# Side-by-side token parts: two matmuls where three stood, and PSUM as four pairs of banks

## The chip, the cores and the metric

The kernel runs on one core of one Trainium2 chip. The metric is the device time of one execution in microseconds (us). The kernel before was timed three times: 933.48, 933.98 and 934.42, a median of 933.98 us. Engines are named as in the profile: PE multiplies matrices (PEld is its loading of the stationary operand, which overlaps PE), DVE and ACT are the two elementwise engines, POOL does some small powers, and SP issues the transfers.

## The reference, cut to what matters

The input is 256 tokens of 1024 features in float32. A first block runs a SwiGLU feed-forward, a token mixer (retention and neighbourhood attention) and a second feed-forward; a second block runs a gated linear recurrence and a gated short convolution. Nearly all the work is in products with weights that are read once:

```python
def _swiglu(x, w_in, w_out):
    g, u = jnp.split(x @ w_in, 2, axis=-1)
    return (jax.nn.silu(g) * u) @ w_out

def first_block(x, ...):
    h = _swiglu(_rms_norm(x, ffn1_pre_norm), ffn1_w_in, ffn1_w_out)     # 1024 -> 2 x 2816 -> 1024
    x = x + 0.5 * _rms_norm(h, ffn1_post_norm)
    x = x + _rms_norm(_token_mixing(_rms_norm(x, mix_pre_norm), w_mix_in, ...), mix_post_norm)
    h = _swiglu(_rms_norm(x, ffn2_pre_norm), ffn2_w_in, ffn2_w_out)
    return x + 0.5 * _rms_norm(h, ffn2_post_norm)

def second_block(x, ...):
    x = x + recurrent_mixer(rmsnorm(x, norm_g[0]), a_w_in, ...)   # 1024 -> 2 x 1536 -> 1024
    x = x + shortconv_mixer(rmsnorm(x, norm_g[1]), b_w_in, ...)   # 1024 -> 4 x 1536 -> 1024
    return rmsnorm(x, final_g)
```

## The kernel before, in words

Every float32 operand of a large product is held as two float32r parts, hi (a rounded copy) and lo (the rest), and a product is three matmuls: hi by hi, hi by lo and lo by hi. The helper `mm3` (lines 222 to 226) issues them for one stationary and one moving pair.

Weights come in parts of 128 by 1024 (512 KB), 300 of which are split: a transfer on SP's queue (L75) fills `raw`, ACT copies `raw` to `hi` (L87), and DVE subtracts to get `lo` (L88). The parts lie in a ring of 41 slots of 4 KB a partition; a part is split up to 15 parts ahead of its use when the ring has room.

A block has two phases. In `phase_a` a unit of 256 output features is made feature-major: the weights are stationary and the 256 tokens are the moving columns (`mm_a2`, 16 calls of `mm3` a unit, 256 columns each, into one PSUM bank). The normed input is a `Pair`: tiles `ph` and `pl`, four K-tiles of 256 tokens to a slot. The first units of a phase are taken token-major instead (`mm_tok`: tokens stationary, 256 weight columns moving) and turned by PE afterwards. In `phase_b` tokens are stationary and 512 columns of weights move (`mm_b`), into four accumulator banks. The token mixer also uses 512 moving columns for its token-major products (`mm_t`).

At the end of a unit the block's `evac` reads the bank: in the feed-forward ACT takes Silu of the gate's bank (L471), DVE multiplies it by the other bank (L472), and `split_pair` makes the next pair (L450, L451). At the joint between blocks the new normed input `hn` is turned by PE and split by `transpose_pair` (L346, L350, L351): four tiles of 128 columns to a bank, one ACT copy and one DVE subtraction of 512 columns for each bank. PSUM is a pool of eight tiles of one bank each.

The program is written in order and a scheduler, fed by a model of the engines, sets the order of each engine's instructions when it is built; an engine runs its own list in that order. In the mixer, DVE adds a mask to four bias tables `t2` (L603), which come by 16 small transfers of `in_na_rel_bias`, and turns queries and keys by position (`rope`, L568 to L573) before PE transposes them (`turn`, L581). In the recurrent block `conv` (L937, L942) reads the bank of a unit, `gates` (L912) multiplies its result by the gate weights, and `finish` (L1004 to L1011) ends in the pairs that `phase_b` reads.

Of the kernel before, what the change touches and what calls it, by code (L numbers as in the profile page):

```python
# [49 lines left out]
class Stream:  # L50
    """Weights in the order of their use: loaded ahead, then split into two float32r parts."""
# [72 lines left out]
def block_kernel(ctx: ExitStack, tc: tile.TileContext, A, C, out):  # L124
# [63 lines left out]
    add(u_ag[:EARLY] + [ax[0], ax[1], u_gw[0], ax[2], u_gw[1], ax[3], ax[4], u_gw[2], ax[5]] + u_ag[EARLY:])  # L188
# [33 lines left out]
    def mm3(ps, a, b, first, last):  # L222
        """ps += a[0]+a[1] times b[0]+b[1], each a pair of float32r parts (stationary, moving)."""
# [4 lines left out]
    class Pair:  # L228
        """A feature-major activation in two float32r parts, by tiles of 128 features."""

        def __init__(self, nk):
            self.nk, self.gone = nk, 0
            self.h, self.l = [], []

        def slots(self, k):
            while k // 4 >= len(self.h):
                self.h.append(S.slot(F32R, "ph"))
                self.l.append(S.slot(F32R, "pl"))

        def at(self, k, t0=0, t1=SEQ):  # L240
            o = (k % 4) * SEQ
            return self.h[k // 4][:, o + t0:o + t1], self.l[k // 4][:, o + t0:o + t1]

        def view(self, part, k, n):
            self.slots(k)
            t = (self.h if part == 0 else self.l)[k // 4]
            o = (k % 4) * SEQ
            return t[:, o:o + n * SEQ].rearrange("p (k t) -> p k t", k=n)

        def used(self, k):  # L250
            """Tiles up to k are done with."""
            while self.gone <= (self.nk - 1) // 4 and (k >= 4 * self.gone + 3 or k == self.nk - 1):
                S.drop(2)
                self.gone += 1
# [3 lines left out]

    def mm_a2(bk, u, xt):
        """bk[features, (half, token)] for the 256 columns of u."""  # L260
        for m in range(2):
            c = slice(m * 128, (m + 1) * 128)
            for q, p in enumerate(u.parts):
                if m == 0:
                    S.use(p)
                for j in range(p.a):
                    k = q * p.a + j
                    mm3(bk[:, m * SEQ:(m + 1) * SEQ], (p.hi[:, j, c], p.lo[:, j, c]), xt.at(k),
                        k == 0, k == u.a - 1)
                if m == 1:  # L270
                    S.done(p)

    def mm_tok(bk, u, xt, t):
        """bk[token of tile t, (t, 256 columns)]"""
# [10 lines left out]
    def mm_t(ps, p, xt, t, k0, nk):  # L285
        """ps[token of tile t, 512 columns], the tiles of K in p"""
# [4 lines left out]
    def columns(*cuts):  # L291
        """accumulators (bank, columns) of a token tile"""
        return [(bank()[:, :b - a], slice(a, b)) for a, b in zip(cuts, cuts[1:])]

    def mm_b(acc, p, xt, t, k, nk):
        """the columns of acc of token tile t, tile k of K"""
# [4 lines left out]
    def inv_rms(a, b, eps):  # L301
        """(a + b + eps) ** -0.5"""
# [37 lines left out]
    def transpose_pair(src, t, pair, k0, n):  # L340
        """n tiles of 128 columns of the token-major src become tiles k0.. of pair, tokens t."""
        for b in range(0, n, 4):
            ps = bank()
# [3 lines left out]
            pv = ps[:, :m * 128].rearrange("p (k t) -> p k t", k=m)  # L347
            h = pair.view(0, k0 + b, m)[:, :, t * 128:(t + 1) * 128]
            lo = pair.view(1, k0 + b, m)[:, :, t * 128:(t + 1) * 128]
            act.activation(out=h, in_=pv, func=AF.Copy)  # L350
            dve.tensor_tensor(out=lo, in0=pv, in1=h.bitcast(F32), op=ALU.subtract)  # L351

    class Next:
        """What a block hands over: its normed input, one token tile after the other."""
# [26 lines left out]
        # (tile, part, columns): the last parts by columns, so that the first columns' sum of  # L381
        # squares runs under the others' products
# [21 lines left out]
    def phase_a(us, nxt, evac, late, tok_evac=None):  # L404
        """feature-major products of the normed input. The first units are taken token-major, token
        tile 0 first, so that the second tile's norm runs under the first's products."""
# [8 lines left out]
        for i, u in enumerate(us):  # L415
# [3 lines left out]
            else:  # L419
                b = bank()  # L420
# [10 lines left out]
    def turn_tok(src):  # L431
        """[token, (tile, 256 features)] to a bank [feature, (half, token)]."""
# [7 lines left out]
    def turn_evac(evac):  # L440
        def first(i, b):
            s = tmp()
            act.activation(out=s, in_=b, func=AF.Copy)
            return lambda: evac(i, turn_tok(s))
        return first

    def split_pair(pair, k, n, src):
        """src [128, n, 256] becomes tiles k..k+n of pair."""
        h, lo = pair.view(0, k, n), pair.view(1, k, n)
# [11 lines left out]
    def ffn(us, nxt, post, next_ap, late, aside=None):  # L461
# [3 lines left out]
        def evac(i, b):  # L465
            if i % 2 == 0:
                held[i] = b
                return
            g = held.pop(i - 1)
            sg = tmp()  # L470
            act.activation(out=sg, in_=g, func=AF.Silu)  # L471
            dve.tensor_tensor(out=sg, in0=sg, in1=b, op=ALU.mult)  # L472
            split_pair(f, i - 1, 2, two(sg))
# [3 lines left out]
        def tok_evac(i, b):  # L477
# [7 lines left out]
            return lambda: split_pair(f, i - 1, 2, two(turn_tok(sg)))  # L485
# [36 lines left out]
    def mixing(nxt):  # L522
        dist = S.slot(F32, "dist")
        S.fetch(dist, C["dist"])
        # rows of the mirrored bias, one further to the right for each query: keys in falling order
# [9 lines left out]
        # queries and keys of the retention, token-major, turned by their positions  # L535
        xt = nxt.pair
        acc = [[bank(), bank()] for _ in range(2)]
# [13 lines left out]
        # decay[m, t] between key m and query t  # L551
# [35 lines left out]
        # neighbourhood queries and keys, feature-major  # L587
        nqk = [S.slot(F32, "nqk") for _ in range(2)]

        def full_a(u, xt):  # L590
            b = bank()
            mm_a2(b, u, xt)
            return b

        for i, u in enumerate(u_nq + u_nk):
            b = full_a(u, xt)
            act.activation(out=nqk[i // 2][:, (i % 2) * 512:(i % 2 + 1) * 512], in_=b, func=AF.Copy,
                           scale=ND ** -0.5 if i < 2 else 1.0)
            turn(roped[i // 2][i % 2], i // 2, i % 2)
# [5 lines left out]
        # scores of the retention, [key, query], weighted by the decay  # L605
# [10 lines left out]
        # scores of the neighbourhood attention, [query, key]  # L616
# [4 lines left out]
        def na_scores(hh, i):  # L621
# [6 lines left out]
            pb = [bank(), bank()]  # L628
# [22 lines left out]
        def full_t(us, xt, evac, between):  # L651
            ps = [bank(), bank()]
# [16 lines left out]
        def bt_nv(i):  # L669
            na_scores(0, i)  # L670
# [27 lines left out]
        def na_turn(h):  # L698
# [8 lines left out]
            if hl == 3:  # L707
                S.drop(2)      # prob
# [6 lines left out]
        def na_pv(h):  # L715
            if h == 0:
                na_o.extend([bank(), bank()])
# [5 lines left out]
            if h % 2:  # L723
                S.drop()       # pt
# [9 lines left out]
        # the retention's output, token-major, normed by heads  # L734
# [4 lines left out]
        def ret_y(t):  # L739
            for hp in range(2):  # L740
                ps = bank()
# [43 lines left out]
        S.drop(4)      # rp, v  # L785
# [11 lines left out]
        def o_turn(i):  # L797
# [3 lines left out]
            pv = ps.rearrange("p (k t) -> p k t", k=4)  # L801
            h, lo = (ot.view(z, 0, 4)[:, :, i * 128:(i + 1) * 128] for z in range(2))
            act.activation(out=h, in_=pv, func=AF.Copy)
            dve.tensor_tensor(out=lo, in0=pv, in1=h.bitcast(F32), op=ALU.subtract)

        for i, u in enumerate(u_gn + u_gr):
            S.reserve = 6 if i < 6 else 4
            b = full_a(u, xt)
# [342 lines left out]
```

## Time and profile before

| what | value |
|---|---|
| median of three runs | 933.98 us |
| the profiled execution, first to last instruction (its span) | 934.7 us |
| PE busy | 910.2 us, 97% of the span |
| PEld busy | 852.6 us, 91% |
| DVE busy | 555.1 us, 59% |
| ACT busy | 470.0 us, 50% |
| PE's share of the chain that ended last | 85% |

The profiled execution has only its span as a time; it is 0.7 us longer than the median. Matmuls overlap in the pipeline, so what one costs is the distance from its start to the next one's start, not the duration in its row.

### The profile page before, as it was taken

What the parts mean: (1) busy time and instruction counts of PE and PEld (TensorE: products, weight loads), DVE (VectorE), ACT (ScalarE), POOL (GpSimd) and SP (SyncE); (2) the same over time, 40 slices, a digit from 0 to 9 for tenths busy, and PEclk for the clock granted to TensorE, in tenths of its full rate; (3) what the DMA queues carried; (4) which work ended last, traced back from release to release, by engine and by line L of the source; (5) the groups of instructions that cost most, each with busy time, mean ns of one, the idle gap of its engine ahead of it and who ended that gap; (6) DMA issues with size and microseconds to landing.
All of it is one profiled execution on the core that took longest, in us unless ns stands there. A gap on an engine that the chain in (4) does not pass through costs nothing.

```text
span 934.7 us, 15517 instructions
## 1 busy us (share of the span) xinstructions
PE 910.2 (97%) x6374; PEld 852.6 (91%) x6374; DVE 555.1 (59%) x714; ACT 470.0 (50%) x662; POOL 13.9 (1%) x24
## 2 busy tenths in 40 slices
PE   5999999999999999999999999999999999999997
PEld 5999998888978899998999999889998889999986
DVE  5774555556936463667574446545787965756512
ACT  6664545443746454545454444534769845544401
POOL 0000000000000000000000000000000000000000
PEclk9999999999999999999999999999999999999999
DMA  9964547747527443666555546767426745655401
GB/s 299 328 209 158 175 158 251 264 116 199 190 86 247 126 150 131 225 201 222 164 182 164 159 165 211 238 190 245 139 91 204 246 154 183 221 163 182 158 1 46
DMA packets 132442, 169.21 MB, mean 181 GB/s; under 512 B 12048, under 2 KB 112148, under 8 KB 132372
## 3 DMA queue, kind: packets, MB, share of 16 engines
q1 hardware_dynamic: 132372, 168.23, 55.8%
q8 instruction: 50, 0.82, 0.4%
q14 instruction: 20, 0.16, 0.1%
HBM read 167.16 MB, written 1.05 MB: 180 GB/s over the span
## 4 chain that ended last, share of the span: by engine, by line
PE 85%; DVE 5%; ACT 4%; DMA 2%; SPq 2%; issue 2%; POOL 0%; DVEq 0%; POOLq 0%; ACTq 0%
PE bank L224 27%; PE bank L226 27%; PE bank L225 27%; DVE lo L88 2%; SPq L116 1%; DMA t<-in_na_rel_bias 1%; DMA raw<-in_ffn_w_in 1%; DVE ri L1008 1%; ACT hi L87 1%; PE bank L721 1%; PE bank L746 1%; ACT ri L949 1%; ACT u L948 0%; PE bank L436 0%; PE bank L632 0%
## 5 line engine op out<-in xcount | busy, mean ns | idle before, releaser
L88 DVE TENSOR_TENSOR lo<-raw,hi 128x1024 fp32r<-128x1024 f32 x300 | 358.9, 1221 | 132.2 <-ACT hi L87 79.8
L87 ACT ACTIVATE hi<-raw 128x1024 fp32r<-128x1024 f32 x300 | 307.0, 1055 | 172.7 <-PE bank L226 69.2
L224 PE MATMUL bank<-ph,hi 128*128 128x256 f32 x1360 | 387.3, 285 | 0.0
L225 PE MATMUL bank<-pl,hi 128*128 128x256 f32 x1360 | 384.9, 283 | 0.0
L226 PE MATMUL bank<-ph,lo 128*128 128x256 f32 x1360 | 384.8, 283 | 0.0
L225 PEld LDWEIGHTS bank<-pl,hi 128*128 128x128 f32 x1360 | 261.0, 192 | 0.2
L224 PEld LDWEIGHTS bank<-ph,hi 128*128 128x128 f32 x1360 | 261.0, 192 | 0.2
L226 PEld LDWEIGHTS bank<-ph,lo 128*128 128x128 f32 x1360 | 261.0, 192 | 0.0
L224 PE MATMUL bank<-hi,ph 128*128 128x512 f32 (+1 forms) x636 | 225.4, 356 | 4.2 <-ACT ph L350 4.2
L225 PE MATMUL bank<-lo,ph 128*128 128x512 f32 (+1 forms) x636 | 223.5, 353 | 0.2 <-DVE lo L88 0.2
L226 PE MATMUL bank<-hi,pl 128*128 128x512 f32 (+1 forms) x636 | 221.7, 353 | 1.9 <-DVE pl L351 1.8
L224 PEld LDWEIGHTS bank<-hi,ph 128*128 128x128 f32 x636 | 121.4, 191 | 23.2 <-ACT ph L350 6.5
L226 PEld LDWEIGHTS bank<-hi,pl 128*128 128x128 f32 x636 | 120.4, 191 | 18.4 <-DVE pl L351 2.6
L225 PEld LDWEIGHTS bank<-lo,ph 128*128 128x128 f32 x636 | 121.4, 191 | 15.8 <-DVE lo L88 0.5
L450 ACT ACTIVATE ph<-tmp 128x512 fp32r<-128x512 f32 x28 | 17.6, 629 | 57.5 <-DVE tmp L472 52.8
L313 ACT ACTIVATE tmp<-x 128x512 f32<-128x512 f32 (+1 forms) x25 | 15.2, 609 | 41.6 <-DVE x L328 34.5
L472 DVE TENSOR_TENSOR tmp<-tmp,bank 128x512 f32<-128x512 f32 x19 | 13.0, 685 | 34.5 <-PE bank L226 34.5
L451 DVE TENSOR_TENSOR pl<-tmp,ph 128x512 fp32r<-128x512 f32 x28 | 19.1, 689 | 12.9 <-ACT ph L450 12.9
L304 DVE TENSOR_SCALAR small<-small 128x1 f32<-128x1 f32 x18 | 3.8, 210 | 34.6 <-ACT tmp L332 28.4
L351 DVE TENSOR_TENSOR pl<-bank,ph 128x512 fp32r<-128x512 f32 x24 | 15.8, 684 | 13.5 <-ACT ph L350 13.5
L306 POOL TENSOR_TENSOR small<-small,half 128x1 f32<-128x1 f32 x18 | 11.7, 650 | 809.8 <-DVE small L304 809.8
L321 DVE SCALAR_TENSOR_TENSOR hn<-x,small,g 128x512 f32<-128x512 f32 x24 | 17.0, 748 | 9.8 <-POOL small L306 6.6
(135 smaller groups left out, 413.4 us busy)
## 6 DMA issues: line engine op xcount, KB each, us to landing
raw<-in_ffn_w_in SPq DMA_DIRECT2D x88, 512.0 KB, 5.2
raw<-in_w_mix_in SPq DMA_DIRECT2D x52, 512.0 KB, 4.5
raw<-in_b_w_in SPq DMA_DIRECT2D x48, 512.0 KB, 4.4
raw<-in_ffn_w_out SPq DMA_DIRECT2D x44, 512.0 KB, 4.3
raw<-in_a_w_in SPq DMA_DIRECT2D x24, 512.0 KB, 4.3
raw<-in_a_w_out SPq DMA_DIRECT2D x12, 512.0 KB, 3.7
raw<-in_b_w_out SPq DMA_DIRECT2D x12, 512.0 KB, 4.0
raw<-in_w_ret_out SPq DMA_DIRECT2D x8, 512.0 KB, 4.3
```

The lines of the kernel that those rows point to most:

```text
L87: self.copied = self.nc.scalar.activation(out=p.hi, in_=p.raw, func=AF.Copy)
L88: self.nc.vector.tensor_tensor(out=p.lo, in0=p.raw, in1=p.hi.bitcast(F32), op=ALU.subtract)
L224: pe.matmul(ps, a[0], b[0], start=first, stop=False)
L225: pe.matmul(ps, a[0], b[1], start=False, stop=False)
L226: pe.matmul(ps, a[1], b[0], start=False, stop=last)
L306: nc.gpsimd.tensor_tensor(out=r, in0=v, in1=half[:, 0:1], op=ALU.pow)
L313: act.activation(out=tmp()[:, :c1 - c0], in_=x[:, t, c0:c1], func=AF.Square, scale=1.0 / 32, accum_out=ss[:, c:c + 1])
L321: dve.scalar_tensor_tensor(out=hn[:, s], in0=x[:, t, s], scalar=r, in1=g[:, s], op0=ALU.mult, op1=ALU.mult)
L351: dve.tensor_tensor(out=lo, in0=pv, in1=h.bitcast(F32), op=ALU.subtract)
L450: act.activation(out=h, in_=src, func=AF.Copy)
L451: dve.tensor_tensor(out=lo, in0=src, in1=h.bitcast(F32), op=ALU.subtract)
L472: dve.tensor_tensor(out=sg, in0=sg, in1=b, op=ALU.mult)
```

## The change: what it does

A `Pair` now keeps the hi and the lo tokens of one K-tile side by side: 256 hi columns and then 256 lo columns, two K-tiles to a slot. `mm_wide` passes a stationary hi weight block over all 512 of them in one matmul, and the lo weight block over the 256 hi columns in a second. The two halves of the result, weights by hi tokens and hi weights by lo tokens, lie in the two halves of a bank, so a unit needs two banks; `total` sums the halves when the unit is evicted, with one ACT copy and one DVE addition into an SBUF tile, and what followed reads that tile. PSUM is a pool of four tiles of two banks; code that wants single banks takes halves of a pair. The ring has 40 slots instead of 41, the pool `tmp` eight tiles instead of six. `transpose_pair` splits two tiles at a time instead of four. In the mixer the transposes of the turned queries and keys come two units later; in the recurrent block the gates come one unit later.

```diff
-RING = 41          # slots of 4 KB a partition
+RING = 40
-    tp = ctx.enter_context(tc.tile_pool(name="tmp", bufs=6))
+    tp = ctx.enter_context(tc.tile_pool(name="tmp", bufs=8))
-    pp = ctx.enter_context(tc.tile_pool(name="psum", bufs=8, space=PSUM))
+    pp = ctx.enter_context(tc.tile_pool(name="psum", bufs=4, space=PSUM))
+    spare = []
+    def double():
+        return pp.tile([128, 2, 512], F32, tag="b", name="bank")
+    def banks2():
+        b = double()
+        return [b[:, 0, :], b[:, 1, :]]
     def bank():
-        return pp.tile([128, 512], F32, tag="b", name="bank")
+        if not spare:
+            spare.extend(banks2())
+        return spare.pop(0)
...
+        def both(self, k):
+            o = (k % 2) * 512
+            return self.s[k // 2][:, o:o + 512]
...
+    def mm_wide(b, w, xt, k, first, last):
+        hi, lo = w
+        pe.matmul(b, hi, xt.both(k), start=first, stop=False, skip_group_check=True)
+        pe.matmul(b[:, 0:SEQ], lo, xt.at(k)[0], start=False, stop=last, skip_group_check=True)
...
     def mm_a2(bk, u, xt):
...
-                    mm3(bk[:, m * SEQ:(m + 1) * SEQ], (p.hi[:, j, c], p.lo[:, j, c]), xt.at(k),
-                        k == 0, k == u.a - 1)
+                    mm_wide(bk[:, m, :], (p.hi[:, j, c], p.lo[:, j, c]), xt, k, k == 0, k == u.a - 1)
...
+    def total(out, bk, scale=None):
+        v = bk.rearrange("p m (z t) -> p m z t", z=2)
+        o = two(out)
+        if scale is None:
+            act.activation(out=o, in_=v[:, :, 1, :], func=AF.Copy)
+            dve.tensor_tensor(out=o, in0=v[:, :, 0, :], in1=o, op=ALU.add)
...
     def transpose_pair(src, t, pair, k0, n):
-        for b in range(0, n, 4):
-            ps = bank()
+        for b, ps in zip(range(0, n, 4), banks2()):
...
+            for j in range(0, m, 2):
+                pv = ps[:, j * 128:(j + 2) * 128].rearrange("p (k t) -> p k t", k=2)
+                h, lo = (pair.view(z, k0 + b + j)[:, :, t * 128:(t + 1) * 128] for z in range(2))
...
         def evac(i, b):                      # feed-forward
             if i % 2 == 0:
-                held[i] = b
+                held[i] = total(tmp(), b)
+                act.activation(out=held[i], in_=held[i], func=AF.Silu)
                 return
-            g = held.pop(i - 1)
-            sg = tmp()
-            act.activation(out=sg, in_=g, func=AF.Silu)
-            dve.tensor_tensor(out=sg, in0=sg, in1=b, op=ALU.mult)
+            sg, u = held.pop(i - 1), total(tmp(), b)
+            dve.tensor_tensor(out=sg, in0=sg, in1=u, op=ALU.mult)
...
         for i, u in enumerate(u_nq + u_nk):  # token mixer
-            b = full_a(u, xt)
...
-            turn(roped[i // 2][i % 2], i // 2, i % 2)
+            full_a(u, xt, nqk[i // 2][:, (i % 2) * 512:(i % 2 + 1) * 512], ND ** -0.5 if i < 2 else None)
+            if i > 1:
+                turn(roped[0][i - 2], 0, i - 2)
...
-        def evac(i, b):                      # recurrent block
+        def evac(i, b, turned=False):
             j = i - EARLY
-            conv(j, b)
-            if j:
-                S.todo.append(partial(sigmoids, j - 1, gates(j - 1)))
+            conv(j, b if turned else total(tmp(), b))
+            if j > 1:
+                S.todo.append(partial(sigmoids, j - 2, gates(j - 2)))
...
             b = double()
             mm_a2(b, u, xt)
-            banks.append(b)
-            if j == 0:
-                S.todo.append(partial(sigmoids, 5, gates(5)))
+            banks.append(total(tmp(), b))
+            if j < 2:
+                S.todo.append(partial(sigmoids, 4 + j, gates(4 + j)))
```

PE's list in a feed-forward unit, before: `hi` and `lo` are the weights (stationary), `ph` and `pl` the token parts (moving), and 128x256 is the output.

```order
L224 MATMUL bank_606<-ph_123,hi_400 128x256
L225 MATMUL bank_606<-pl_124,hi_400 128x256
L226 MATMUL bank_606<-ph_123,lo_401 128x256
L224 MATMUL bank_606<-ph_123,hi_400 128x256
L225 MATMUL bank_606<-pl_124,hi_400 128x256
L226 MATMUL bank_606<-ph_123,lo_401 128x256
```

And in such a unit now, where `pr` holds both token parts:

```order
L279 MATMUL bank_492<-pr_133,hi_374 128x512
L280 MATMUL bank_492<-pr_133,lo_375 128x256
L279 MATMUL bank_492<-pr_133,hi_374 128x512
L280 MATMUL bank_492<-pr_133,lo_375 128x256
L279 MATMUL bank_492<-pr_136,hi_374 128x512
L280 MATMUL bank_492<-pr_136,lo_375 128x256
```

Two matmuls stand for three; the program has 1360 such pairs where it had 1360 such triples, and all other matmuls are as many as before.

DVE's list where the token mixer begins, before: L603 adds the mask to a bias table, L351 subtracts for `pl` of the second token tile (its eight K-tiles in two instructions), L88 splits weights, L555 begins the decay tables.

```order
L603 TENSOR_TENSOR t2_2174<-t2_2174,mask_79 128x768
L351 TENSOR_TENSOR pl_2119<-bank_2264,ph_2118 128x4x128
L351 TENSOR_TENSOR pl_2128<-bank_2271,ph_2127 128x4x128
L603 TENSOR_TENSOR t2_2175<-t2_2175,mask_79 128x768
L88 TENSOR_TENSOR lo_2201<-raw_2079,hi_2200 128x1024
L88 TENSOR_TENSOR lo_2207<-raw_2091,hi_2206 128x1024
```

The same place now (L637 is the mask, L387 the subtraction, in four instructions for the second token tile, L590 the decay tables):

```order
L637 TENSOR_TENSOR t2_1910<-t2_1910,mask_79 128x768
L88 TENSOR_TENSOR lo_1933<-raw_1810,hi_1932 128x1024
L637 TENSOR_TENSOR t2_1911<-t2_1911,mask_79 128x768
L387 TENSOR_TENSOR pr_1861<-bank_1994,pr_1861 128x2x128
L88 TENSOR_TENSOR lo_1939<-raw_1822,hi_1938 128x1024
L88 TENSOR_TENSOR lo_1949<-raw_1828,hi_1948 128x1024
L590 TENSOR_SCALAR decay_2059<-dist_1906,lg_96 128x512 x2
L590 TENSOR_SCALAR decay_2060<-dist_1906,lg_96 128x512 x2
L387 TENSOR_TENSOR pr_1864<-bank_1994,pr_1864 128x2x128
```

The last two subtractions of the second token tile (K-tiles 4 to 7) stood ahead of the last mask and now stand behind it, the very last one also behind two splits and four decay instructions.

## Rows read from the trace of the kernel before

**Rows 1.** Page, part 1: busy time, share of the span, count.

```profile
PE 910.2 (97%) x6374; PEld 852.6 (91%) x6374; DVE 555.1 (59%) x714; ACT 470.0 (50%) x662; POOL 13.9 (1%) x24
```

**Rows 2.** Page, part 4: the chain that ended last, by engine.

```profile
PE 85%; DVE 5%; ACT 4%; DMA 2%; SPq 2%; issue 2%; POOL 0%; DVEq 0%; POOLq 0%; ACTq 0%
```

**Rows 3.** Groups by shape: busy us, mean ns of one, idle us before it.

```profile
L224 PE MATMUL bank<-ph,hi 128*128 128x256 f32 x1360 | 387.3, 285 | 0.0
...
L88 DVE TENSOR_TENSOR lo<-raw,hi 128x1024 fp32r<-128x1024 f32 x300 | 358.9, 1221 | 132.2 <-ACT hi L87 79.8 <-PE bank L225 33.2 <-issue 15.0
```

**Rows 4.** Timeline of PE, 59.8 to 64: start, duration, line, operation.

```profile
59.77 0.28 PE L225 MATMUL bank<-pl,hi 128*128 128x256 f32 x1
...
63.97 0.28 PE L224 MATMUL bank<-ph,hi 128*128 128x256 f32 x1
```

**Rows 5.** Timeline of PE, 599.7 to 602.

```profile
599.66 0.39 PE L226 MATMUL bank<-hi,pl 128*128 128x512 f32 x1
...
601.93 0.39 PE L224 MATMUL bank<-hi,ph 128*128 128x512 f32 x1
```

**Rows 6.** Timeline of PE, 896 to 898, where widths change.

```profile
896.42 0.39 PE L226 MATMUL bank<-hi,pl 128*128 128x512 f32 x1
896.65 0.28 PE L224 MATMUL bank<-hi,ph 128*128 128x256 f32 x1
...
897.24 0.28 PE L226 MATMUL bank<-hi,pl 128*128 128x256 f32 x1
897.36 0.40 PE L224 MATMUL bank<-hi,ph 128*128 128x512 f32 x1
```

**Rows 7.** Timeline of PE, 442 to 444: float32 transposes.

```profile
442.23 0.93 PE L346 MATMUL bank<-ident,hn 128*128 128x128 f32 x7
```

**Rows 8.** Waits of PE: us in total, times, longest.

```profile
PE bank L224 <- ACT ph L350: 4.2, 9, 1.1
PE bank L226 <- DVE pl L351: 1.8, 2, 1.0
PE bank L581 <- DVE tmp L573: 1.6, 1, 1.6
PE bank L912 <- DVE u L942: 0.9, 1, 0.9
```

**Rows 9.** Groups by shape: instructions like the added ones.

```profile
L350 ACT ACTIVATE ph<-bank 128x512 fp32r<-128x512 f32 x24 | 13.1, 594 | 17.3 <-PE bank L346 17.3
L472 DVE TENSOR_TENSOR tmp<-tmp,bank 128x512 f32<-128x512 f32 x19 | 13.0, 685 | 34.5 <-PE bank L226 34.5
...
L328 DVE TENSOR_TENSOR x<-bank,x 128x256 f32<-128x256 f32 x2 | 0.8, 424 | 1.0 <-PE bank L226 1.0
L313 ACT ACTIVATE tmp<-x 128x256 f32<-128x256 f32 x2 | 0.8, 418 | 1.4 <-DVE x L328 1.4
```

**Rows 10.** Timeline of PE, 203 to 232: the token mixer's first product.

```profile
205.37 0.50 PE L224 MATMUL bank<-hi,ph 128*128 128x512 f32 x1 [0.45 <-ACT ph L350]
```

**Rows 11.** Timeline of DVE, 218 to 232: in brackets the idle time before.

```profile
218.85 0.96 DVE L603 TENSOR_TENSOR t<-t,mask 128x768 f32<-128x768 f32 x1 [0.40 <-DMA t<-in_na_rel_bias]
...
225.97 0.96 DVE L603 TENSOR_TENSOR t<-t,mask 128x768 f32<-128x768 f32 x1 [4.96 <-DMA t<-in_na_rel_bias]
226.84 3.48 DVE L88 TENSOR_TENSOR lo<-raw,hi 128x1024 fp32r<-128x1024 f32 x3
230.25 1.66 DVE L555 TENSOR_SCALAR decay<-dist,lg 128x512 f32<-128x512 f32 x4
```

**Rows 12.** Timeline of PE, 695 to 718: recurrent block.

```profile
695.57 1.68 PE L912 MATMUL bank<-u,raw 128*128 128x256 f32 x7
...
717.47 0.40 PE L224 MATMUL bank<-hi,ph 128*128 128x512 f32 x1
```

**Rows 13.** Timeline of DVE, 703 to 735: recurrent block.

```profile
703.54 0.86 DVE L942 SCALAR_TENSOR_TENSOR u<-bank,vec_a,u 128x253 f32<-128x253 f32 x2
...
729.02 1.89 DVE L451 TENSOR_TENSOR pl<-tmp,ph 128x512 fp32r<-128x512 f32 x3
```

More of the change, by code (lines that the diff above doesn't have):

```diff
@@ L232, in __init__, with slot, view @@
             self.nk, self.gone = nk, 0
[L233 to L238, printed above, removed]
-        def at(self, k, t0=0, t1=SEQ):
[L241 to L248, printed above, removed]
+            self.s = []
+        def slot(self, k):
+            while k // 2 >= len(self.s):
+                self.s.append(S.slot(F32R, "pr"))
+            return self.s[k // 2]
+        def at(self, k, t0=0, t1=SEQ):
+            t, o = self.s[k // 2], (k % 2) * 512
+            return t[:, o + t0:o + t1], t[:, o + SEQ + t0:o + SEQ + t1]
+        def both(self, k):
+            o = (k % 2) * 512
+            return self.s[k // 2][:, o:o + 512]
+        def view(self, part, k):
+            return self.slot(k).rearrange("p (k z t) -> p k z t", k=2, z=2)[:, :, part, :]
         def used(self, k):
-            while self.gone <= (self.nk - 1) // 4 and (k >= 4 * self.gone + 3 or k == self.nk - 1):
-                S.drop(2)
+            while self.gone <= (self.nk - 1) // 2 and (k >= 2 * self.gone + 1 or k == self.nk - 1):
+                S.drop()
                 self.gone += 1
@@ L291, in columns @@
     def columns(*cuts):
-        return [(bank()[:, :b - a], slice(a, b)) for a, b in zip(cuts, cuts[1:])]
+        bs = banks2()
+        if len(cuts) > 3:
+            bs += banks2()
+        return [(ps[:, :b - a], slice(a, b)) for ps, a, b in zip(bs, cuts, cuts[1:])]
     def mm_b(acc, p, xt, t, k, nk):
@@ L419, in phase_a @@
             else:
-                b = bank()
+                b = double()
                 mm_a2(b, u, xt)
@@ L484, in tok_evac @@
             dve.tensor_tensor(out=sg, in0=sg, in1=b, op=ALU.mult)
[L485 removed]
+            return lambda: split_pair(f, i - 1, two(turn_tok(sg)))
         xt = phase_a(us[0], nxt, evac, late, tok_evac)
@@ L536, in mixing @@
         xt = nxt.pair
-        acc = [[bank(), bank()] for _ in range(2)]
+        acc = [banks2() for _ in range(2)]
         qk_units = [u_rq, u_rk]
@@ L627, in na_scores @@
             tv = [t2[2 * hh + q][:, :768].rearrange("p (h r c) -> p h r c", h=2, r=6) for q in range(2)]
-            pb = [bank(), bank()]
+            pb = banks2()
             for hl in range(4):
@@ L651, in full_t @@
         def full_t(us, xt, evac, between):
-            ps = [bank(), bank()]
+            ps = banks2()
             parts = [p for u in us for p in u.parts]
@@ L716, in na_pv @@
             if h == 0:
-                na_o.extend([bank(), bank()])
+                na_o.extend(banks2())
             for i in range(2):
@@ L739, in ret_y @@
         def ret_y(t):
-            for hp in range(2):
-                ps = bank()
+            for hp, ps in enumerate(banks2()):
                 ybk[t, hp] = ps
@@ L800, in o_turn @@
                 pe.transpose(ps[:, j * 128:(j + 1) * 128], otok[i][:, j * 128:(j + 1) * 128], ident)
[L801 to L804, printed above, removed]
+            for j in (0, 2):
+                pv = ps[:, j * 128:(j + 2) * 128].rearrange("p (k t) -> p k t", k=2)
+                h, lo = (ot.view(z, j)[:, :, i * 128:(i + 1) * 128] for z in range(2))
+                act.activation(out=h, in_=pv, func=AF.Copy)
+                dve.tensor_tensor(out=lo, in0=pv, in1=h.bitcast(F32), op=ALU.subtract)
         for i, u in enumerate(u_gn + u_gr):
             S.reserve = 6 if i < 6 else 4
-            b = full_a(u, xt)
-            act.activation(out=sg(i // 4, i % 4), in_=b, func=AF.Sigmoid)
+            b = full_a(u, xt, sg(i // 4, i % 4))
+            act.activation(out=b, in_=b, func=AF.Sigmoid)
             if i < 2:
@@ L824, in mixing @@
         for i, u in enumerate(u_no):
-            b = [bank(), bank()]
+            b = [double(), double()]
             for m in range(4):
@@ L838, in mixing @@
                 s = sg(0, 2 * i + mp)
-                dve.tensor_tensor(out=s, in0=s, in1=b[mp], op=ALU.mult)
+                dve.tensor_tensor(out=s, in0=s, in1=total(tmp(), b[mp]), op=ALU.mult)
         ot.drop()
@@ L846, in mixing @@
             dve.tensor_tensor(out=s, in0=s, in1=sg(0, i), op=ALU.add)
-            split_pair(mg, 2 * i, 2, two(s))
+            split_pair(mg, 2 * i, two(s))
             if i % 2:
@@ L904, in gates @@
             got = []
-            for hh in range(2):
+            for hh, ps in enumerate(banks2()):
                 h = 2 * j + hh
@@ L1001, in finish @@
             else:
-                g = tmp()
+                g = banks[j - EARLY]
                 with after("sqrt"):
-                    act.activation(out=g, in_=banks[j - EARLY], func=AF.Silu)
+                    act.activation(out=g, in_=g, func=AF.Silu)
             rv = pair_view(j)
@@ L1010, in finish @@
             dve.tensor_tensor(out=two(g), in0=two(g), in1=rv[:, :, 0, :], op=ALU.mult)
-            split_pair(y, 2 * j, 2, two(g))
+            split_pair(y, 2 * j, two(g))
             S.drop()
@@ L1038, in shortconv, with evac @@
         held = []
-        def evac(i, b):
-            held.append(b)
-            if i % 4 != 3:
+        def evac(i, b, turned=False):
+            z = i % 4
+            if turned:
+                got = b
+            else:
+                got = total(tmp(), b)
+            if z == 0 and turned:
+                held.append(tmp())
+                act.activation(out=held[0], in_=got, func=AF.Copy)
+                return
+            held.append(got)
+            if z == 1:
+                dve.tensor_tensor(out=held[0], in0=held[0], in1=got, op=ALU.mult)
+            if z < 3:
                 return
             j = i // 4
-            cg, xv, bg, gt = held
+            w, _, bg, gt = held
             held.clear()
-            w = tmp()
-            act.activation(out=w, in_=cg, func=AF.Copy)
-            dve.tensor_tensor(out=w, in0=w, in1=xv, op=ALU.mult)
             o = tmp()
@@ L1061, in evac @@
                                              op0=ALU.mult, op1=ALU.add)
-            sg = tmp()
+            sg = tmp() if turned else gt
             act.activation(out=sg, in_=gt, func=AF.Silu)
@@ L1065, in evac @@
             dve.tensor_tensor(out=o, in0=o, in1=sg, op=ALU.mult)
-            split_pair(y, 2 * j, 2, two(o))
+            split_pair(y, 2 * j, two(o))
         xt = phase_a([u for us in u_b for u in us], nxt, evac, LATE_A)
```

42 lines of the change are left out of this document (21 added, 21 removed).

## The prediction

> **What bounds the kernel now.** I read the page's busy times first, then the chain that ended last, the groups by shape, PE's timeline in three stretches, and last the waits of PE and the timelines around them. In the first the reader is to see that PE is busy 910.2 of 934.7 us, 97%, while DVE has 59% and ACT 50% [rows 1]; in the second that PE makes up 85% of the chain [rows 2]. Both say that time comes only from shorter matmul work, or from PE's few waits. PE's busy time is full of overlap, so a matmul's price has to be read as the distance between starts. With 256 moving columns, 35 distances lie between 59.77 and 63.97 [rows 4]: 4.20/35 = 0.120 us. With 512, 10 lie between 599.66 and 601.93 [rows 5]: 0.227 us. The difference, 0.107 us, is what 256 more columns cost; so a matmul costs 0.107 us per 256 columns and 0.0133 us (120.0 − 106.7 ns) whatever its width. Read at 60, at 600 and at 896 us [rows 4 to 6], the distances fit one list of prices for the whole run.
>
> **The matmuls.** The triple of three 256-column matmuls costs 3 × 120 = 360 ns. The pair passes the same 768 columns in two instructions: 227 + 120 = 346.7 ns, one fixed part less. This form is not in the trace, but its changes of width are: a 512 followed by a 256 took 0.23 (896.42 to 896.65), a 256 followed by a 512 took 0.12 (897.24 to 897.36) [rows 6], 0.35 for the two. The program has 1360 such triples [rows 3] and now 1360 pairs: 1360 × 13.3 ns = **−18.1 us**. Bounds: nothing is gained if the pair still costs 360; and the float32 transposes, also short matmuls, start (0.93 − 0.27)/6 = 0.109 us apart [rows 7] (0.27 is the duration of one, an estimate from the 0.28 of the 256-column rows); if the narrow matmul of a pair came down to that, the gain would be 1360 × 24.3 ns = −33 us. I take the middle value because the rows nearest to the new form, the changes of width, give it.
>
> The Trainium skill ("TensorE: Matmul & The Clock Gate", section "Back-to-back issue gap") gives the isolated gap as the columns at 2.4 GHz plus 2.5 ns. By that the fixed part is a fifth of what rows 4 and 5 show, and 1360 fewer of them would be an estimated −3.4 us; the float32 transposes of rows 7 agree with it, the products that this change touches do not.
>
> **The work added beside PE.** 87 evictions get a `total`: one ACT copy of 512 columns, like L350 at 594 ns, and one DVE addition from PSUM, like L472 at 685 ns [rows 9]: 51 us more on ACT, 60 on DVE. The 24 evictions of transposes become 48 of half the width: DVE 48 × 0.424 − 24 × 0.685 = +4, ACT 48 × 0.418 − 24 × 0.594 = +6 [rows 9]. ACT comes to some 525 us and DVE to 619, at most 68% of the new span. PE hides both as long as banks come free in time. A unit is 16 pairs, 5.55 us; with four pairs of banks the next use of a pair comes three units, 16.6 us, after its end. The eviction itself takes 594 + 685 ns, and one split of 1221 ns [rows 3] may stand ahead of it: some 2.5 us. The longest that I found a bank held before was 8.8 us, from 695.57 to 704.40, when `conv` had read it [rows 12, 13]. So I cost the totals at nothing; without that cover each would cost its 1.3 us, 111 us in all.
>
> **Waits that go.** The turned queries wait 1.6 us once for `rope`'s last instruction, and the gates 0.9 us once for `conv` [rows 8]; two units and one unit later (11 and 5.5 us) both find their operand: −1.6 and −0.9. The product after a joint's transposes waits for an ACT copy of 512 columns, 4.2 us in nine times [rows 8]. A copy of half the width is 594 − 418 = 176 ns shorter [rows 9]: eight joints and tiles × about 0.15 = −1.2. Late next is the DVE subtraction behind it, 0.26 us shorter too.
>
> **Where the mixer begins** is the first place that may lose. Take its first product, 205.37 [rows 10], as zero. In DVE's new list the low part of K-tiles 4 and 5 of the second token tile stands behind the last mask; before, both subtractions stood ahead of it. The last bias landed at 225.97 [rows 11], that is at 20.6. Mask (0.9) and subtraction (0.42) make those tiles ready at 22.0. PE has 76 matmuls of 512, 4 pairs and 12 transposes ahead of their first use: 76 × 0.227 + 4 × 0.347 + 12 × 0.109 = 19.9. A stall of 2.1. K-tiles 6 and 7 stand behind two more splits and four decay instructions (2 × 1.16 + 1.66 from 226.84 and 230.25 [rows 11]) and a subtraction: ready at 26.4, while PE wants them 12 matmuls and 2 pairs later, at 23.3 + 2.1 = 25.4: 1.0 more. Behind them on DVE wait only splits. Together 3.1 in place of 0.9, half of the 1.8 that PE waited for `pl` before [rows 8]: **+2.2**. Bounds: −1 if the last bias comes 3 us earlier; +8 if it lands as much later as DVE's idle wait for it was here, 4.96 [rows 11].
>
> **Other places that may lose.** In the mixer's query and key units two accumulator banks of the rotation and one transposed pair now take whole pairs of banks: a unit may wait for one; from nothing to 2, I take +1.0. At the end of the recurrent block nine totals put 9 × 0.685 = 6.2 us on DVE in a stretch where its work sets the end: the last `y` pairs were ready at 729.02 + 1.89 = 730.9 [rows 13], and `phase_b`, begun at 717.47 [rows 12], wants the seventh of its K-tiles after 6 × 12 matmuls of 0.227 = 16.3 us, at 733.8. The lead is 2.9, so 0 if the totals fit into idle time, 3.3 if none does and the rest of the block stays, 6.2 if the lead is gone too; I take +1.5, about the middle of the first two. The four transposes each that stand apart now bring changes between float32 and float32r products, at most 0.2 us each by the 0.50 that the first product lasts beside 0.39 of its like [rows 5, 10]: six more at 0.11, +0.7.
>
> **Sum.** −18.1 − 1.6 − 0.9 − 1.2 + 2.2 + 1.0 + 1.5 + 0.7 = −16.4. From the span of 934.7 that gives 918.3; the median of the runs is 0.7 below this span, so **917.6 us**.
>
> **Rivals.**
> *Stalls twice or three times as long.* Mixer and recurrent block at their upper bounds: +5.8 and +4.7 more, 922 to 928. For it: DVE's new list does put late work ahead of what PE wants. Against: only two places have so short a lead.
> *The pair is cheaper.* If the narrow matmul runs under its neighbour at the 109 ns of the transposes, another 11 ns each, −15: 903. For: rows 7. Against: 896.42 to 897.36 [rows 6] shows no such gain where widths change.
> *The fixed part does not go with the number of matmuls* but with the columns or the stationary operand, and only 2.5 ns of it is the instruction's: the 109 ns of rows 7 leave just 2.3 over the streaming time. Then −3.4, and with the other terms −1.7: 932, no measurable change. Against: rows 4 and 5 have the same 13.3 at both widths. (That is the rule of the skill named above.)
> *Slower: banks come too late.* Each of the 85 wide units waits for a pair of banks, since ACT and DVE take their splits first: `total` stands in the same queues, two engines one after the other, where one reading was enough. It decides from 16.4/85 = 0.19 us a unit; at 0.5 us (half a split of 1221 ns less the slack) it costs 42 − 16 = 26 more: 960; at 0.3, 943. For: a pair is now a quarter of PSUM, where a unit took an eighth. Against: DVE is idle 41% of the time [rows 1], and 2.5 us stand against 16.6.
>
> **Chances.** Forecast (912 to 922) 0.63; longer stalls 0.18; cheaper pair 0.07; fixed part kept 0.04; banks too late 0.06; the remaining 0.02 is a mix near 930. A change under 0.2%, 1.9 us, can't be told from none. Faster: 0.63 + 0.18 + 0.07 + 0.02 = 0.90, the same 0.04, slower 0.06. For 8 in 10 the range takes the forecast, most of the longer stalls and a part of the cheaper pair: 909 to 927.
>
> **What would show it.** In the profile after: wide starts followed by the narrow one 0.227 later and by the next wide one 0.120 after that; the wait for the rope's instruction and the one for `conv` gone; a wait of PE for `pr` of 2 to 3 us at the mixer's start; no waits of the wide matmul for `total`'s reader; DVE near 619 and ACT near 525 us busy. I am wrong if the pair's two distances don't add to 347, if PE waits for a bank in many units, or if a single stall is longer than 5 us.

## The result, and the profile after

The change makes the kernel slower: 960.32 us (959.22 to 961.70, four runs) against 934.20 us for the kernel before, a ratio of 1.0271 (95% interval 1.0249 to 1.0293). The forecast was 917.6 us, 909 to 927, and faster with a chance of 0.90. The profiled execution of the kernel after has a span of 959.9 us.

The page's part 1 and the chain by engine, of the kernel after:

```profile
PE 912.4 (95%) x5014; PEld 787.0 (82%) x5014; DVE 613.9 (64%) x827; ACT 514.3 (54%) x768; POOL 13.0 (1%) x24
...
PE 84%; DVE 5%; ACT 5%; DMA 2%; issue 1%; SPq 1%; POOL 0%; DVEq 0%; POOLq 0%; ACTq 0%
```

The 1360 matmuls fewer show (5014 for 6374), and DVE and ACT grew to 614 and 514 us, near the forecast 619 and 525. But PE's busy time, against [rows 1], did not fall, and its share did: the time went into short waits and into products that ran slowly. PE's waits in the kernel after, in total, times and longest, for comparison with [rows 8]:

```profile
PE bank L382 <- DVE hn L358: 15.7, 3, 7.7
PE bank L236 <- ACT pr L386: 5.4, 6, 1.5
PE bank L279 <- DVE tmp L301: 3.3, 1, 3.3
PE bank L236 <- ACT tmp L798: 2.9, 1, 2.9
PE bank L238 <- DVE pr L387: 2.2, 3, 1.3
PE bank L236 <- ACT pr L486: 2.2, 1, 2.2
PE bank L382 <- DVE pr L387: 1.9, 2, 1.6
```

L382 are the transposes of the normed input at a joint, L386 and L387 the copy and the subtraction that read them. Only the third row is a wait of the wide matmul (L279) for a `total` (L301); the others stand at the program's start or where phases meet. I added up, over all of PE's instructions, by how much the distance from one start to the next is longer than the price list (120 ns for 256 columns, 227 for 512, 110 for 128):

| us above the price list | before | after | single banks (below) |
|---|---|---|---|
| waits, each above 0.3 us | 12.1 | 38.7 | 13.4 |
| products at about half rate | 6.2 | 14.8 | 7.3 |
| wide pairs and other products at full rate | -0.1 | 6.8 | 6.9 |
| the rest (float32 products, changes of type) | 7.9 | 10.2 | 12.6 |

After minus before is 44.4 us; less the 18.1 us of fixed parts saved that is 26.3, and with the first transposes 1.3 us earlier (7.75 for 9.04) 25.0, against 25.3 between the spans.

The second line of the table grows by 8.6 us. Some 6.4 of them lie in three stretches, at 451 to 457, 751 to 758 and 775 to 782, in which the granted clock was 0.50; the kernel before shows none ahead of its last microseconds. The second of them, in the kernel after at the end of the recurrent block: the seventh figure, ahead of DMA's share, is the granted clock.

```profile
745.00:749.00 4.00, 2.40 (x11) 1.67 (x9) 4.00 (x8) 3.11 (x6) 0.00 (x0) 1.00 0.30 99
749.00:752.00 3.00, 1.25 (x5) 0.73 (x5) 3.00 (x6) 1.86 (x4) 0.00 (x0) 0.81 0.22 78
752.00:754.00 2.00, 2.00 (x5) 1.61 (x6) 2.00 (x3) 2.00 (x3) 0.00 (x0) 0.50 0.90 296
...
757.00:760.00 3.00, 3.00 (x13) 2.38 (x12) 3.00 (x4) 3.00 (x4) 0.00 (x0) 0.88 0.45 155
```

PE is busy 2.40 of 4 us, then 1.25 of 3, as it waits for the last pairs; the clock falls from 1.00 (2.4 GHz) to 0.50 (1.2 GHz), and within the last row, with PE fully busy again, it returns to 1.00 (the 0.88 is the mean of the row). In between, the products of 512 columns start 0.43 us apart (752.54, 752.97) where [rows 5] had 0.227; the twelve of them cost 2.4 us on top of the waits.

### The profile page after: what moved, and what is told of

It is laid out like the page before. It is cut to its first block, busy times and chain, and to the rows that moved or that the text cites. A ratio compares the mean times of both kernels' runs of the same rounds, so it can differ in the third digit from the quotient of the medians.

```text
span 959.9 us, 12882 instructions
## 1 busy us (share of the span) xinstructions
PE 912.4 (95%) x5014; PEld 787.0 (82%) x5014; DVE 613.9 (64%) x827; ACT 514.3 (54%) x768; POOL 13.0 (1%) x24
## 4 chain that ended last, share of the span: by engine, by line
PE 84%; DVE 5%; ACT 5%; DMA 2%; issue 1%; SPq 1%; POOL 0%; DVEq 0%; POOLq 0%; ACTq 0%
PE bank L279 31%; PE bank L280 16%; PE bank L238 11%; PE bank L236 11%; PE bank L237 11%; DVE lo L88 2%; SPq L116 1%; ACT hi L87 1%; DMA t<-in_na_rel_bias 1%; PE bank L382 1%; DVE ri L1042 1%; PE bank L756 1%; DMA raw<-in_ffn_w_in 1%; ACT ri L961 1%; PE bank L780 1%
## 5 line engine op out<-in xcount | busy, mean ns | idle before, releaser
L279 PE MATMUL bank<-pr,hi 128*128 128x512 f32 x1360 | 482.1, 399 | 3.3 <-DVE tmp L301 3.3
L88 DVE TENSOR_TENSOR lo<-raw,hi 128x1024 fp32r<-128x1024 f32 x300 | 357.5, 1220 | 68.9 <-ACT hi L87 60.5
L280 PE MATMUL bank<-pr,lo 128*128 128x256 f32 x1360 | 381.9, 281 | 0.0
L279 PEld LDWEIGHTS bank<-pr,hi 128*128 128x128 f32 x1360 | 255.4, 188 | 64.6 <-DVE tmp L301 3.7
L280 PEld LDWEIGHTS bank<-pr,lo 128*128 128x128 f32 x1360 | 256.9, 189 | 0.4
L236 PE MATMUL bank<-hi,pr 128*128 128x512 f32 (+1 forms) x636 | 229.6, 362 | 12.8 <-ACT pr L386 5.4
L238 PE MATMUL bank<-hi,pr 128*128 128x512 f32 (+1 forms) x636 | 225.5, 361 | 3.4 <-DVE pr L387 2.2
L237 PE MATMUL bank<-lo,pr 128*128 128x512 f32 (+1 forms) x636 | 227.4, 359 | 1.1 <-DVE lo L88 1.1
L236 PEld LDWEIGHTS bank<-hi,pr 128*128 128x128 f32 x636 | 124.3, 196 | 33.5 <-ACT pr L386 7.6
L238 PEld LDWEIGHTS bank<-hi,pr 128*128 128x128 f32 x636 | 122.9, 195 | 21.7 <-DVE pr L387 4.0
L237 PEld LDWEIGHTS bank<-lo,pr 128*128 128x128 f32 x636 | 124.2, 195 | 17.3 <-DVE lo L88 1.7
L300 ACT ACTIVATE tmp<-bank 128x512 f32<-128x512 f32 x75 | 44.7, 597 | 95.1 <-PE bank L280 95.0
L301 DVE TENSOR_TENSOR tmp<-bank,tmp 128x512 f32<-128x512 f32 x75 | 51.5, 687 | 66.3 <-ACT tmp L300 66.2
L386 ACT ACTIVATE pr<-bank 128x256 fp32r<-128x256 f32 x48 | 18.2, 380 | 43.8 <-PE bank L382 32.0
L382 PE MATMUL bank<-ident,hn 128*128 128x128 f32 x80 | 14.7, 318 | 17.6 <-DVE hn L358 15.7
L387 DVE TENSOR_TENSOR pr<-bank,pr 128x256 fp32r<-128x256 f32 x48 | 20.1, 421 | 17.5 <-ACT pr L386 17.3
L487 DVE TENSOR_TENSOR pr<-tmp,pr 128x512 fp32r<-128x512 f32 x28 | 19.2, 691 | 15.6 <-ACT pr L486 15.5
L382 PEld LDWEIGHTS bank<-ident,hn 128*128 128x128 f32 x80 | 11.1, 164 | 19.6 <-issue 8.8
```

Of the source, the lines that this page charges most:

```text
L88: self.nc.vector.tensor_tensor(out=p.lo, in0=p.raw, in1=p.hi.bitcast(F32), op=ALU.subtract)
L236: pe.matmul(ps, a[0], b[0], start=first, stop=False)
L237: pe.matmul(ps, a[0], b[1], start=False, stop=False)
L238: pe.matmul(ps, a[1], b[0], start=False, stop=last)
L279: pe.matmul(b, hi, xt.both(k), start=first, stop=False, skip_group_check=True)
L280: pe.matmul(b[:, 0:SEQ], lo, xt.at(k)[0], start=False, stop=last, skip_group_check=True)
```

## The experiments

Two theories stood at the start. Theory A: what costs is PSUM as pairs. A pair is one tile, and an instruction on one half waits for readers and writers of the other. Theory B: what costs is the second reading of every unit, which makes evictions late, as my rival of late banks had it.

**Single banks.** The changed kernel with eight tiles of one bank; a wide unit takes two.

```diff
-    pp = ctx.enter_context(tc.tile_pool(name="psum", bufs=4, space=PSUM))
-    spare = []
+    pp = ctx.enter_context(tc.tile_pool(name="psum", bufs=8, space=PSUM))
...
     def double():
...
+        return [bank(), bank()]
+
+    banks2 = double
...
+        for m in range(2):
+            om, h, r = o[:, m, :], bk[m][:, 0:SEQ], bk[m][:, SEQ:512]
+            if scale is None:
+                act.activation(out=om, in_=r, func=AF.Copy)
+                dve.tensor_tensor(out=om, in0=h, in1=om, op=ALU.add)
...
```

> The changed kernel with PSUM as eight tiles of one bank again: a wide unit takes two such tiles, and its total is two ACT copies and two DVE additions of 256 columns. Theory A (two banks that share a tile wait for each other's readers and writers, which lengthens the chains at every joint): the 26.7 us of added PE waits fall by about 20, the clock's share by about 5: 930 to 938 us, transposes of a joint again eight in a row. Theory B (the second reading of each unit makes evictions late, whatever the tile): the waits stay, the extra instructions make them no shorter: 955 to 965.

Measured: 931.87 us, 0.9947 of before (0.9931 to 0.9964). It does more work on DVE and ACT (622 and 524 us) than the changed kernel, and is 28 us faster. Its waits:

```profile
PE bank L376 <- DVE hn L352: 13.8, 3, 8.6
PE bank L229 <- ACT pr L480: 2.3, 1, 2.3
PE bank L230 <- DVE lo L88: 1.1, 2, 0.7
PE bank L231 <- DVE pr L381: 0.7, 1, 0.7
PE bank L272 <- ACT ri L955: 0.6, 1, 0.6
```

The rows of the copies and subtractions behind a joint are nearly gone (8.6 us of the 13.8 are the start of the program, which had 9.0 before). Theory A's range holds, and theory B's 955 to 965 is out. How a pair delays shows at two places. First the sums of squares (ACT's L369, L363 in this kernel) of the two accumulators of a token tile. The kernel after, ACT at 439, and the kernel of single banks at a joint like it:

```profile
439.07 0.60 ACT L369 ACTIVATE tmp<-bank 128x512 f32<-128x512 f32 x1 [3.51 <-PE bank L238]
439.56 0.19 ACT L369 ACTIVATION_READ_ACCUMULATOR tmp<-bank 128x1 f32 x1
439.66 0.59 ACT L369 ACTIVATE tmp<-bank 128x512 f32<-128x512 f32 x1
```

```profile
622.07 0.60 ACT L363 ACTIVATE tmp<-bank 128x512 f32<-128x512 f32 x1 [1.85 <-PE bank L231]
622.56 0.19 ACT L363 ACTIVATION_READ_ACCUMULATOR tmp<-bank 128x1 f32 x1
624.73 0.60 ACT L363 ACTIVATE tmp<-bank 128x512 f32<-128x512 f32 x1 [1.98 <-PE bank L231]
```

With single banks the first sum runs while PE fills the second bank, 2.66 us ahead. As a pair, both wait for the last product, and what stands behind them on ACT is 0.6 us late (439.07 to 439.66). Second, the transposes. PE at the joint ahead of the mixer in the kernel after, and at the joint ahead of the recurrent block with single banks:

```profile
206.56 0.60 PE L382 MATMUL bank<-ident,hn 128*128 128x128 f32 x4
208.41 0.50 PE L236 MATMUL bank<-hi,pr 128*128 128x512 f32 x1 [1.25 <-ACT pr L386]
...
212.18 0.60 PE L382 MATMUL bank<-ident,hn 128*128 128x128 f32 x4
```

```profile
624.53 1.03 PE L376 MATMUL bank<-ident,hn 128*128 128x128 f32 x8
625.74 0.39 PE L229 MATMUL bank<-hi,pr 128*128 128x256 f32 x1 [0.18 <-ACT pr L380]
```

Eight in a row became four and, 5.6 us later, four: the second four write the other half of the pair and come behind the reading of the first (the row L382 <- L387 above is PE waiting for that). Both are waits of the program: as built, the kernel after has the first sum wait for the last product into the other half, and the second four transposes for the subtraction that reads the first four. The chip did not need them: with single banks the first sum ran beside those products.

**The kernel before with pairs, nothing else.**

```diff
-    pp = ctx.enter_context(tc.tile_pool(name="psum", bufs=8, space=PSUM))
+    pp = ctx.enter_context(tc.tile_pool(name="psum", bufs=4, space=PSUM))
+    spare = []
...
-        return pp.tile([128, 512], F32, tag="b", name="bank")
+        if not spare:
+            b2 = pp.tile([128, 2, 512], F32, tag="b", name="bank")
+            spare.extend([b2[:, 0, :], b2[:, 1, :]])
+        return spare.pop(0)
```

> The kernel before with one edit: PSUM as four tiles of two banks, single banks being halves of one. No wide matmul, no total. Theory A: most of the added waits appear here, 15 to 30 us: 950 to 964. Theory B: nothing is evicted later, so within 5 us of before: 930 to 939.

Measured: 976.71 us, 1.0422 (1.0393 to 1.0451), 41 us slower without one `total`, more than I expected. Its waits begin so:

```profile
PE bank L350 <- DVE hn L325: 12.9, 2, 9.0
PE bank L228 <- ACT ph L354: 6.9, 9, 1.7
PE bank L916 <- ACT ri L953: 4.6, 1, 4.6
PE bank L916 <- DVE u L946: 4.4, 1, 4.4
PE bank L228 <- ACT ri L931: 3.7, 2, 1.9
```

The gates (L916), whose banks are halves like all others here, wait 9 us; in the kernel after, with a pair of their own and a unit later, they do not wait. Here two users that follow each other by chance share a pair, so the 41 us are not the price of the pairs in the kernel after; they show that pairs without a single `total` can cost as much.

**Transposes in two pairs.** The changed kernel; the two groups of four go to halves of two pairs.

```diff
-        for b, ps in zip(range(0, n, 4), banks2()):
+        for b, ps in zip(range(0, n, 4), [double()[:, 0, :] for _ in range(2)]):
```

> The changed kernel with one edit: the two groups of four transposes of a joint go to two pairs of banks, one half of each, in place of the two halves of one pair. Theory A at this place only: the second group no longer waits for the first one's readers (1.9 us of waits of the transposes for the subtraction, and most of the 5.4 us for the copy behind a joint), 3 to 8 us are saved: 952 to 957. If the accumulators and the order that the lists take from them make the waits, nothing: 958 to 962.

Measured: 956.08 us, 1.0213 (1.0189 to 1.0237): 4 us saved, as theory A has it. The eight stand in a row, the wait for L387 ahead of them is gone, and that for the copy falls from 5.4 us to 1.9, while the products' wait for the subtraction grows from 2.2 to 3.5:

```profile
204.84 1.04 PE L382 MATMUL bank<-ident,hn 128*128 128x128 f32 x8
206.70 0.50 PE L236 MATMUL bank<-hi,pr 128*128 128x512 f32 x1 [0.82 <-ACT pr L386]
```

The 0.82 that stays is the two sums of squares, still one behind the other, ahead of the copy on ACT. So this place is about a seventh of the pairs' 28 us. No experiment divides the rest, but the waits of the table do by place: of the 25.3 us that single banks take away, 3.6 lie in the first 30 us, 1.7 at the mixer's start, 4.6 at its end (316.7 and 322.4), 4.2 at 445 to 452, 3.5 at 641 to 663, 2.5 at the `total` of 725, 1.6 at 749 to 753, 2.3 at 775 to 778 and 1.3 at 802.

**Three narrow matmuls, with pairs and with single banks.** The same edit on the changed kernel and on the kernel of single banks:

```diff
-        pe.matmul(b, hi, xt.both(k), start=first, stop=False, skip_group_check=True)
+        h, r = xt.at(k)
+        pe.matmul(b[:, 0:SEQ], hi, h, start=first, stop=False, skip_group_check=True)
+        pe.matmul(b[:, SEQ:512], hi, r, start=False, stop=False, skip_group_check=True)
```

> The changed kernel with the wide matmul undone: hi weights by hi tokens and by lo tokens as two matmuls of 256 columns, into the same halves of the same banks; everything else stays. If the pair costs the 353 ns read from its starts and the triple 360, it is 1360 x 7 = 9 us slower than the changed kernel, 969; if the joints hide it, less; if the pair were worth the forecast 13.3 ns, 18 us slower, 978.

> The kernel of single banks with the wide matmul undone: three matmuls of 256 columns into the same two banks. Here no joint hides or adds anything: 1360 x (360 - 353.3) = 9 us more than with the pair: 940 to 943, slower than before by 5 to 7 us, the price of all the rest of the change. If the pair is worth 13.3 ns, 950; if it is worth nothing, 932.

Measured: 971.40 us (1.0372, 1.0346 to 1.0398) and 941.85 us (1.0063, 1.0041 to 1.0085). The wide matmul is worth 11 us with pairs and 10 without, each good to about 3: real, and a little over half of the forecast 18.1. That the joints hide it or add to it does not show. The second figure is also the price of everything else in the change, without pairs and without the wide matmul: 6 us over before.

**Four wide, then four narrow.**

```diff
-    def mm_wide(b, w, xt, k, first, last):
...
-        pe.matmul(b, hi, xt.both(k), start=first, stop=False, skip_group_check=True)
-        pe.matmul(b[:, 0:SEQ], lo, xt.at(k)[0], start=False, stop=last, skip_group_check=True)
+    def mm_wides(b, p, c, xt, k0, nk):
+        for j in range(p.a):
+            k = k0 + j
+            pe.matmul(b, p.hi[:, j, c], xt.both(k), start=k == 0, stop=False, skip_group_check=True)
+        for j in range(p.a):
+            k = k0 + j
+            pe.matmul(b[:, 0:SEQ], p.lo[:, j, c], xt.at(k)[0], start=False, stop=k == nk - 1,
+                      skip_group_check=True)
...
```

> The changed kernel with four wide matmuls and then the four narrow ones of a part, in place of wide and narrow in turn. If the 6.4 ns by which a pair costs more than 346.7 come from the change of width (two a pair, now two in four pairs), 1360 x 6.4 x 3/4 = 6.5 us are saved: 953 to 955. If they are the price of writing the same half of a bank twice in a row or of the other engines' traffic, nothing: 958 to 962.

Measured: 959.88 us, 1.0246 (1.0224 to 1.0267), no difference from the changed kernel. A wide product now starts 234.7 ns after a wide one in the mean of the 993 distances under 0.35 us, a narrow one 119.4 after a narrow one: 354 together again. So the change of width is not what a pair costs more. The 6.6 ns by which it misses the forecast 346.7 are of another kind: PE's starts in the kernel after at 60 us and at 130 us, in the same feed-forward:

```profile
60.11 0.40 PE L279 MATMUL bank<-pr,hi 128*128 128x512 f32 x1
60.35 0.28 PE L280 MATMUL bank<-pr,lo 128*128 128x256 f32 x1
...
61.17 0.40 PE L279 MATMUL bank<-pr,hi 128*128 128x512 f32 x1
```

```profile
129.68 0.39 PE L279 MATMUL bank<-pr,hi 128*128 128x512 f32 x1
129.91 0.28 PE L280 MATMUL bank<-pr,lo 128*128 128x256 f32 x1
...
130.72 0.39 PE L279 MATMUL bank<-pr,hi 128*128 128x512 f32 x1
```

Three pairs take 1.06 us at the first place and 1.04 at the second, 353.3 and 346.7 ns each. The granted clock is 1.00 at both. The first rhythm holds for most of the program; in this feed-forward it changed at 119 us, where float32 transposes of another kind (L902, per-channel vectors) came between. With single banks the same transposes, at 109 and 113 us, left it at 353.3. What chooses it stays open.

**Early gates.** The kernel of single banks with the gates and their place among the weights as before the change.

```diff
...
-            if j > 1:
-                S.todo.append(partial(sigmoids, j - 2, gates(j - 2)))
-            if j == 4:
+            if j:
+                S.todo.append(partial(sigmoids, j - 1, gates(j - 1)))
+            if j == 3:
...
```

> The kernel of single banks with the recurrent block's gates again one unit earlier, as in the kernel before. Its waits of 3.9 us for hn and 2.3 us for the last pair, with the slow clock behind them, come from the decay chain that now begins one unit (5.5 us) later: if so, the second token tile again leaves 36 products for the norm, 4 to 8 us are saved, and the gates wait 1 to 2 us for conv: 925 to 929. If the totals on DVE make that chain late, not its start, 930 to 934.

Measured: 933.67 us over twelve runs, 0.9972 (0.9959 to 0.9986): nothing gained. Its median is 1.8 us above that of the later gates, hardly more than the two intervals tell apart. Its waits:

```profile
PE bank L376 <- DVE hn L352: 11.0, 3, 7.7
PE bank L940 <- DVE u L970: 6.7, 2, 4.5
```

The wait for `hn` before the last block fell from 3.9 to 2.1 us and that for the last pair is gone, as I thought; but the gates now wait 6.7 us for `conv`, where I had allowed 1 to 2: with `total` ahead of it `conv`, as I read it, ends later. Here the totals do cost, and the change's later gates lose nothing by it.

## Why the prediction was wrong

The steps in the order of the prediction:

- *The matmuls, -18.1.* Right mechanism, size too large. The pair saves one fixed part, but in the kernel after a wide start is followed by the narrow one after 235.8 ns (the mean of the 1350 distances under 0.35 us) and that by the next wide one after 117.3, 353.1 in all and not 346.7: 1360 x 6.9 = 9.4 us saved, and the two experiments give 10 and 11. I had the price from single changes of width [rows 6], which do repeat (346.7 ns at 130 us), but a row of such pairs mostly falls into the slower rhythm. By the 2.5 ns of the Trainium skill ("TensorE: Matmul & The Clock Gate", section "Back-to-back issue gap") the gain would have been an estimated 3.4; the runs are above it. That the transposes leave only 2.3 ns, as the rival of a kept fixed part says, holds for float32 products: in the kernel before, the gates (L912, 256 columns) start 216 ns apart and the transposes (128 columns) 109, so 128 columns cost 107 and 2 are left. The products that the change touches are float32r.
- *Work beside PE at no cost, "as long as banks come free in time".* This step failed. I checked one thing, whether a unit's pair comes back within three units, and that held but once: a wide matmul waited for a `total` 3.31 us at 725.15, behind six scans on DVE. What I put at nothing is that the pair is the unit of waiting for everyone, transposes and accumulators too: the kernel of single banks, with the same wide matmuls and totals, is 28 us faster. The change of the pool stood in the diff, and in PE's list the eight transposes stood as four and four; I took that for a question of data types (+0.7). The other added work, without pairs and without the wide matmul, costs 6 us and not nothing.
- *Waits that go, -3.7.* The rope's wait and that of the gates are gone. The copy of half the width is shorter (0.38 us), but PE waited 5.4 us for it, where it had waited 4.2 before, as ACT reached it later.
- *The mixer's start, +2.2.* The stall was forecast at 3.1; the row there is 0.46 us at 233.10. The last mask began at 227.57, 19.2 us after the phase's first product at 208.41, where 20.6 was forecast, and PE came to the last K-tiles 24.2 us after it, where 23.3 was forecast. The mixer's loss lay elsewhere: its end, for which I had no term, has 4.2 us of new waits (1.29 at 316.70, 2.89 at 322.38).
- *The recurrent block's end, +1.5.* Too small: 2.2 and 1.1 us of waits and 2.4 of slow clock. With single banks 2.3 us stay, and with the gates early again they go, so this part is the totals with the later gates, not the pairs.
- *No term for the joint itself.* PE waited 3.39 us for the norm of the first token tile ahead of 448.77, and 4.59 us ahead of the last block:

```profile
444.99 0.39 PE L238 MATMUL bank<-hi,pr 128*128 128x512 f32 x1
448.77 0.63 PE L382 MATMUL bank<-ident,hn 128*128 128x128 f32 x4 [3.39 <-DVE hn L358]
...
774.96 1.08 PE L382 MATMUL bank<-ident,hn 128*128 128x128 f32 x4 [4.59 <-DVE hn L358]
```

At the first of them, some 10 us of sums, power and scaling lie between the end of the first tile's products and these transposes. Before, 45 products of the second tile (10.2 us) covered them in PE's list; now 28 are left (6.4 us), because the list takes others of them earlier; with single banks 38, and the wait is 1.26 us. At the second, single banks still wait 3.86 us and the early gates with them 2.05, so most of that is not the pairs. The lists were at hand before the result.

Of the rivals, "banks come too late", at 0.06, had the sign, and that its 960 is the measured time is luck: not 85 small waits at units, but some twenty, most of them where phases meet. "Longer stalls" had one place right, the recurrent block's end, and too small a size, 922 to 928, because I let two stalls grow and the clock not fall. Of my three signs of being wrong only the first showed (353 for 347); neither waits for banks in many units nor a new stall over 5 us did, so the signs were not aimed at the step that failed.

In sum, by medians (the kernel before stood at 934 beside the kernel after and at 936 beside the experiments, so each part is good to some 3 us): before 936; all of the change but the pairs and the wide matmul +6; the wide matmul -10; PSUM as pairs +28; together 960. The kernel of single banks keeps the gain and drops the pairs: at 931.87 us it is faster than both, by 0.5% than before.

## What to carry to other kernels

Before making buffers larger, list everything that takes from the same pool, not only the code that wanted them: two banks in one tile made their users wait for each other's halves, and that cost three times what the wide matmul gave. Where a joint hangs on a chain of some 10 us, count in the new list how many products are left to cover it. And a stall can cost more than its length: in three places the clock fell to 0.50 behind waits, and the products there took some 6.4 us more.

## What was not expected of the hardware

The same alternation of 512 and 256 columns, at a granted clock of 1.00, ran at 353.3 ns a pair in some stretches and 346.7 in others of the same program, steadily for tens of us each. What chooses between them stays open.

The granted clock fell to 0.50 behind the waits at 749 to 752, where PE was busy 2.40 of 4 us and then 1.25 of 3. At a joint of the kernel before, two waits of 0.75 and 0.95 us (ahead of 751.93 and 754.10), with PE busy 1.39 of 3 us between two fuller stretches (the second figure of each row), left it at 1.00:

```profile
748.00:751.00 3.00, 3.00 (x19) 2.49 (x17) 2.55 (x5) 0.53 (x2) 0.53 (x1) 1.00 0.50 163
751.00:754.00 3.00, 1.39 (x10) 1.01 (x8) 3.00 (x5) 1.89 (x5) 0.00 (x0) 1.00 0.96 303
754.00:757.00 3.00, 2.90 (x24) 2.90 (x25) 2.58 (x6) 3.00 (x6) 0.55 (x1) 1.00 0.69 238
```
